# A two-layer hyena, attention and mLSTM model on one core: the recorded stages' issue orders and buffer slots derived anew

## The chip, the cores and the metric

The kernel runs on 1 core of one Trainium2 chip. The metric is the device time of one launch in microseconds (us), as the median of three runs: 1537.01 us for the kernel before, between 1536.03 and 1537.13. Engines are called PE (TensorE, matmuls), DVE (VectorE), ACT (ScalarE), POOL (GpSimd) and SP (SyncE, which here issues nearly all DMA transfers).

## The reference

Two layers run over 512 tokens ("lat") and 256 context tokens ("ctx"), 1024 wide, in fp32. Each layer normalizes its input, scales and shifts it by a modulation of the conditions, mixes, and adds the normalized and gated result. Cut to what matters:

```python
for layer in range(2):
    sh_l, sc_l, ga_l = adaln(c, w_mod[layer], b_mod[layer])      # silu(c) @ w_mod + b_mod, in three parts
    sh_c, sc_c, ga_c = adaln(c_ctx, w_mod[layer], b_mod[layer])
    h_lat = rms_norm(x_lat, g_pre[layer]) * (1 + sc_l) + sh_l    # and h_ctx likewise
    y_lat, y_ctx = even_mixer(...) if layer == 0 else odd_mixer(...)
    x_lat = x_lat + ga_l * rms_norm(y_lat, g_post[layer])        # and x_ctx in layer 0
# even: h @ w_in -> hyena (short conv, gate, long conv by transform) and attention with 8 heads on 2;
#       [hyena * silu(g1), attention * silu(g2)] @ w_out
# odd:  h @ w_in -> mLSTM forward and backward (8 heads, chunks), sum * sigmoid(o), head norm, * silu(z), @ w_out
```

## The kernel before, in words

All large products are emulated in higher precision: each operand is split into a high and a low part (`split`, lines 1024 to 1026: a cast on ACT, then a subtraction on DVE), and `mm3` (line 1034) issues three matmuls, high by high, high by low and low by high, into one PSUM tile.

Weights stream in slices of 256 columns. `load_w` (line 1041) fetches a slice in two halves of 512 KB through three raw buffers (`wr`) and splits each into one of two slots of `wh` and `wl`. While PE reads one slot, the other is refilled. Activations stand in `hTh` and `hTl`, one tile for 512 or 256 tokens.

The modulation is computed by `mod_row`, 256 columns at a time:

```python
for kt in range(KT):
    g = 32 * (kt % 4)
    TE.matmul(ps[g:g + 32], cond[:, kt, :], w[kt], start=kt < 4, stop=kt >= 4)
```

Here `cond` holds the conditions, padded to 32 columns. So each such group is eight plain fp32 matmuls that use a quarter of the array's columns each, in the rows of the profile `128*32`; `w` is an unsplit slice of `w_mod`, held in the place of a `wh` slot (`raw_w`, line 1099). All other matmuls in these stages use the array's full width.

The kernel has seven stages, issued one after the other: "start" (conditions, first norm, first projections), "hy" (hyena), "att" (attention), "out0" (output product of layer 0, its epilogue, and the first transposes of layer 1), "l1a" and "l1b" (layer 1's projections and mLSTM) and "out1" (its output product and epilogue). In a stage `record` (line 1009) only notes the instructions down as the code states them. `play` (line 1014) then issues them by a list of numbers written out in the table `ORDERS` (line 163), and pins that order on every engine:

```python
for i in ORDERS.get(name) or range(len(work)):
    e, fn, a, k = work[i].work
    x = fn(*a, **k)
```

Every engine works its own instructions off in that order, and waits on semaphores where it needs another engine's result or a buffer. Which of a pool's buffers a tile takes is in a second table, `SLOTS` (line 747): `T` (line 949) looks the n-th tile of a tag up there. The PSUM tiles `pj` and `pm` take their slots so, as do `wr`, `xt` and many work tiles. Since every recorded call is issued from one place, nearly all instructions of the profile carry the line 1019.

Of the kernel before, what the change touches and what calls it, by code (L numbers as in the profile page):

```python
# [8 lines left out]
F32R = mybir.dt.float32r  # L9
# [5 lines left out]
P = 128  # L15
# [8 lines left out]
def _hilo(a):  # L24
    """float64 -> two float32 arrays of 12-bit significands whose sum carries 24 bits."""
    a = np.asarray(a, np.float64)

    def r12(v):
        m, e = np.frexp(v)
        return np.ldexp(np.rint(m * 4096.0) / 4096.0, e)  # L30

    hi = r12(a)
    lo = r12(a - hi)
    return hi.astype(np.float32), lo.astype(np.float32)


def _tables():
# [12 lines left out]
    # rotary tables  # L50
# [9 lines left out]
    # hyena positional features, decays and transform matrices, tokens ordered phase by phase  # L60
# [18 lines left out]
    fwd = np.stack([np.cos(ph), -np.sin(ph)], 2)  # tau, r, 2, k  # L79
    iv = np.stack([np.cos(ph), -np.sin(ph)], 2).transpose(3, 1, 2, 0) / NL  # k, r, 2, tau  # L80
    # forward blocks (r, c), then inverse blocks: for c and r = 0, 1 those of r, r + 2 and -(r + 2)
    inv3 = np.stack([iv[:, 0:2], iv[:, 2:4], -iv[:, 2:4]], 3).transpose(0, 2, 1, 3, 4)  # k, c, r, 3, tau
# [5 lines left out]
def _cols(v):  # L88
    """[.., n*128] -> [128, n] columns"""
    v = np.asarray(v)  # L90
    return v.reshape(-1, P).T


def _layout(i):
    """inputs laid out for the device; values unchanged"""
# [16 lines left out]
    def quarters(w):  # L112
        """[1024, 1024] -> [2 groups of 4 k-tiles, 2 column halves, 128, 4 * 512] in the form of a slice"""
        return np.ascontiguousarray(w.reshape(2, 4, P, 2, 512).transpose(0, 3, 2, 1, 4)).reshape(2, 2, P, KT, 256)
# [39 lines left out]
# columns of vecs  # L154
# [3 lines left out]
class Ctx:  # L158
# [3 lines left out]
# the order in which the instructions noted down in a part of the kernel are issued  # L162
# [581 lines left out]
    ],  # L744
}
# which of its buffers a tile takes, by tag and pool
SLOTS = {
    "xt@0": [
        0, 5, 3, 4, 2, 1, 5, 0, 3, 4, 1, 2,
# [6 lines left out]
    ],  # L756
    "ss@0": [
        0, 5, 1, 2, 3, 4,
    ],
    "sst@0": [  # L760
        0, 5, 4, 1, 2, 3,
# [1886 lines left out]
```

## Time and profile before

| what | value |
|---|---|
| median of three runs | 1537.01 us (1536.03 to 1537.13) |
| span of the profiled execution | 1533.4 us |
| between the span and that median | 3.6 us |
| PE busy | 1499.6 us, 98% |
| DVE, ACT, POOL busy | 64%, 47%, 3% |
| HBM traffic | 96 GB/s over the span |

The span runs from the first instruction to the last of one profiled execution. Busy times are sums over an engine's instructions; since matmuls are pipelined and their ends modelled, the step from one matmul's start to the next is a better measure of its cost than its duration. In rows of the timeline the first two numbers are start and duration in us, `x16` counts instructions that a row joins (a plain fp32 matmul shows as two), and brackets name the idle time before a row and who ended it. The stages lie, by PE, at 8.0 to 51.1 us (start), 51.1 to 423.5 (hy), 423.5 to 737.7 (att), 737.7 to 875.3 (out0), 875.3 to 923.5 (l1a), 923.5 to 1434.5 (l1b) and 1434.5 to 1533.4 (out1).

### The profile page before, as it was taken

What the parts mean: (1) busy time and instruction counts of PE and PEld (TensorE: products, weight loads), DVE (VectorE), ACT (ScalarE), POOL (GpSimd) and SP (SyncE); (2) the same over time, 40 slices, a digit from 0 to 9 for tenths busy, and PEclk for the clock granted to TensorE, in tenths of its full rate; (3) what the DMA queues carried; (4) which work ended last, traced back from release to release, by engine and by line L of the source; (5) the groups of instructions that cost most, each with busy time, mean ns of one, the idle gap of its engine ahead of it and who ended that gap; (6) DMA issues with size and microseconds to landing.
All of it is one profiled execution on the core that took longest, in us unless ns stands there. A gap on an engine that the chain in (4) does not pass through costs nothing.

```text
span 1533.4 us, 26152 instructions
## 1 busy us (share of the span) xinstructions
PE 1499.6 (98%) x10652; PEld 1380.3 (90%) x10652; DVE 988.5 (64%) x1947; ACT 716.9 (47%) x1554; POOL 51.7 (3%) x93
## 2 busy tenths in 40 slices
PE   7999999999999999999999899999999999999997
PEld 4889999889999999989988789999999999999885
DVE  6688786877866666684237755665656565666435
ACT  6643444434435454463225566545545453545332
POOL 1000000000000000000001200000000000000000
PEclk9999999999999999999999999999999999999999
DMA  9421211221130111443442402211221232213741
GB/s 375 138 71 51 78 65 51 71 72 39 40 122 29 38 67 61 156 141 105 175 168 97 147 28 87 67 58 63 97 73 56 73 97 73 70 66 104 257 168 69
DMA packets 42625, 148.13 MB, mean 97 GB/s; under 512 B 4928, under 2 KB 7625, under 8 KB 39946
## 3 DMA queue, kind: packets, MB, share of 16 engines
q1 hardware_dynamic: 38968, 137.12, 25.9%
q0 software_dynamic: 1648, 7.01, 1.4%
q10 hardware_dynamic: 1890, 2.34, 0.5%
q8 instruction: 84, 1.38, 0.3%
q14 instruction: 35, 0.29, 0.1%
HBM read 131.77 MB, written 14.68 MB: 96 GB/s over the span
## 4 chain that ended last, share of the span: by engine, by line
PE 93%; ACT 2%; DVE 2%; issue 1%; DMA 1%; SPq 0%; POOL 0%; POOLq 0%; DVEq 0%; ACTq 0%
PE pj L1019 77%; PE pm L1019 14%; PE s L1019 2%; ACT wh L1019 1%; DMA dfb<-y_scratch 1%; DMA xt<-in_x 0%; DVE wl L1019 0%; DVE hTl L1019 0%; ACT hf L1019 0%; ACT hTh L1019 0%; ACT q L1019 0%; DVE hf L1019 0%; DVE xn L1019 0%; DVE xnT L1019 0%; SPq L1019 0%
## 5 line engine op out<-in xcount | busy, mean ns | idle before, releaser
L1019 PE MATMUL pj<-wh,hTh 128*128 128x256 f32 (+1 forms) x1536 | 442.9, 289 | 3.3 <-ACT wh L1019 3.0
L1019 PE MATMUL pj<-wl,hTh 128*128 128x256 f32 (+1 forms) x1536 | 438.3, 285 | 3.2 <-DVE wl L1019 2.1
L1019 PE MATMUL pj<-wh,hTl 128*128 128x256 f32 (+1 forms) x1536 | 437.8, 285 | 0.0
L1019 PEld LDWEIGHTS pj<-wh,hTh 128*128 128x128 f32 x1536 | 290.0, 189 | 9.4 <-ACT wh L1019 4.3
L1019 PEld LDWEIGHTS pj<-wl,hTh 128*128 128x128 f32 x1536 | 291.5, 190 | 6.6 <-DVE wl L1019 4.3
L1019 PEld LDWEIGHTS pj<-wh,hTl 128*128 128x128 f32 x1536 | 290.9, 189 | 1.4
L1019 PE MATMUL pj<-hTh,wh 128*128 128x512 f32 (+1 forms) x832 | 287.1, 345 | 0.0
L1019 PE MATMUL pj<-hTh,wl 128*128 128x512 f32 (+1 forms) x832 | 285.3, 343 | 0.5 <-DVE wl L1019 0.5
L1019 PE MATMUL pj<-hTl,wh 128*128 128x512 f32 (+1 forms) x832 | 285.3, 343 | 0.5 <-DVE hTl L1019 0.5
L1019 DVE TENSOR_TENSOR wl<-wr,wh 128x1024 fp32r<-128x1024 f32 x148 | 180.1, 1218 | 77.4 <-ACT wh L1019 77.1
L1019 ACT CAST wh<-wr 128x1024 fp32r<-128x1024 f32 x148 | 154.1, 1049 | 72.4 <-PE pj L1019 49.3
L1019 PEld LDWEIGHTS pj<-hTh,wl 128*128 128x128 f32 x832 | 156.7, 188 | 21.2 <-DVE wl L1019 0.9
L1019 PEld LDWEIGHTS pj<-hTh,wh 128*128 128x128 f32 x832 | 156.8, 188 | 19.2 <-issue 0.8
L1019 PEld LDWEIGHTS pj<-hTl,wh 128*128 128x128 f32 x832 | 156.8, 188 | 19.0 <-DVE hTl L1019 0.8
L1019 DVE TENSOR_TENSOR PTl<-pj,PTh 128x384 fp32r<-128x384 f32 (+1 forms) x80 | 40.9, 523 | 21.5 <-ACT PTh L1019 21.4
L1019 ACT CAST PTh<-pj 128x384 fp32r<-128x384 f32 (+1 forms) x80 | 35.1, 459 | 40.9 <-PE pj L1019 38.5
L1019 DVE SCALAR_TENSOR_TENSOR C<-C,apb,pj 128x258 f32<-128x258 f32 x64 | 30.6, 479 | 31.2 <-PE pj L1019 30.2
L1019 DVE TENSOR_TENSOR Cl<-C,Ch 128x258 fp32r<-128x258 f32 x64 | 26.8, 423 | 37.1 <-ACT Ch L1019 36.8
L1019 DVE SCALAR_TENSOR_TENSOR num<-pm,cq,num 128x258 f32<-128x258 f32 x64 | 30.2, 480 | 25.4 <-PE pm L1019 10.9
L1019 PE MATMUL pm<-Rh,dfa 128*128 128x256 f32 (+1 forms) x192 | 44.7, 304 | 0.0
L1019 DVE TENSOR_REDUCE mx<-s 128x1 f32<-128x768 f32 (+1 forms) x48 | 36.9, 771 | 11.2 <-PE s L1019 11.2
L1019 DVE TENSOR_TENSOR med<-big 128x512 f32<-128x512 f32 (+1 forms) x48 | 40.4, 864 | 4.8 <-ACT big L1019 4.6
(341 smaller groups left out, 2725.3 us busy)
## 6 DMA issues: line engine op xcount, KB each, us to landing
wr<-in_o_w_in SPq DMA_DIRECT2D x64, 512.0 KB
wr<-in_e_w_in SPq DMA_DIRECT2D x52, 512.0 KB
wh<-in_w_mod SPq DMA_DIRECT2D x18, 1024.0 KB
wr<-in_e_w_out SPq DMA_DIRECT2D x16, 512.0 KB
wr<-in_o_w_out SPq DMA_DIRECT2D x16, 512.0 KB
xt<-in_x SPq DMA_DIRECT2D x12, 512.0 KB
y_scratch<-y SPq DMA_DIRECT2D x8, 512.0 KB
xt<-in_w_mod SPq DMA_DIRECT2D x6, 512.0 KB
```

Source lines behind the costliest of these rows:

```text
L1019: x = fn(*a, **k)
```

## The change

The two tables are replaced; nothing else of the code's statements differs. `ORDERS["start"]` stays as it was. In the other six stages the same numbers stand in another order: 3158 recorded instructions in hy, 3143 in att, 1037 in out0, 426 in l1a, 5281 in l1b and 675 in out1. On the average an instruction moves by 30 to 40 places, at most by several hundred. `SLOTS` has new slots for nearly every tag. Instructions, transfers and buffers are the same in kind and number. The line of the calls becomes 1022, as the tables are three lines longer. A line of each table's diff:

```diff
-        0, 5, 3, 4, 2, 1, 5, 0, 3, 4, 1, 2,
+        2, 3, 1, 4, 5, 0, 3, 2, 1, 0, 4, 5,
...
-        0, 2, 1, 0, 2, 1, 0, 2, 1, 0, 2, 1, 0, 2, 1, 0, 2, 1, 0, 2, 1, 0, 2, 1, 0, 2, 1, 0, 2, 1, 0, 2, 1, 0, 2, 1, 0, 2, 1, 0, 2, 1, 0, 2, 1, 0, 2,
+        2, 0, 2, 1, 1, 0, 1, 0, 1, 2, 1, 0, 2, 1, 0, 2, 0, 2, 1, 0, 0, 2, 2, 0, 1, 2, 0, 0, 2, 1, 0, 2, 2, 0, 2, 1, 0, 1, 2, 1, 0, 2, 0, 2, 0, 1, 1,
```

The first place is on PE near the end of att, around one group of modulation matmuls (`pj_4816<-wh_1174,cond`; `PTh`, `PTl` are the attention's weights, `hTh`, `hTl` the activations). Before:

```order
L1019 MATMUL pj_4814<-PTh_4807,hw_1049 128x256
L1019 MATMUL pj_4814<-PTl_4808,hw_1049 128x256
L1019 MATMUL pj_4814<-PTh_4807,ab_1050 128x256
L1019 MATMUL pj_4816<-wh_1174_4810,cond_67 32x256 x8
L1019 MATMUL pj_4815<-wh_1129_4765,hTh 128x256
L1019 MATMUL pj_4815<-wl_1130_4766,hTh 128x256
```

And now:

```order
L1022 MATMUL pj_4806<-PTh_4792,hw_1049 128x256
L1022 MATMUL pj_4816<-wh_1174_4810,cond_67 32x256 x4
L1022 MATMUL pj_4806<-PTl_4793,hw_1049 128x256
L1022 MATMUL pj_4813<-wh_1129_4765,hTl 128x256
L1022 MATMUL pj_4816<-wh_1174_4810,cond_67 32x256
L1022 MATMUL pj_4806<-PTh_4792,ab_1050 128x256
L1022 MATMUL pj_4816<-wh_1174_4810,cond_67 32x256
L1022 MATMUL pj_4821<-wh_1129_4765,hTl 128x256
L1022 MATMUL pj_4816<-wh_1174_4810,cond_67 32x256
L1022 MATMUL pj_4821<-wh_1129_4765,hTh 128x256
```

The group of eight, once together, is now dealt out among products of three other tiles; its last matmul follows some rows further down. Of the 16 groups outside the first stage 16 runs stood on PE before (8 in att, 4 in out0, 4 in out1), and 43 stand now (26, 10 and 7).

The second place is on PE in the first part of l1b, where a projection tile `pj_10005`, the mLSTM's sums `pm_9997`, and the next projection tile `pj_10019` stand. Before:

```order
L1019 MATMUL pj_10005<-wl_1695_9963,hTh 128x256
L1019 MATMUL pj_10005<-wh_1694_9962,hTl 128x256
L1019 MATMUL pm_9997<-Ch_9988,qh_9948 128x258
L1019 MATMUL pm_9997<-Cl_9989,qh_9948 128x258
L1019 MATMUL pm_9997<-Ch_9988,ql_9949 128x258
L1019 MATMUL pj_10019<-wh_1700_9968,hTh 128x256
```

And now:

```order
L1022 MATMUL pm_9997<-Cl_9989,qh_9948 128x258
L1022 MATMUL pj_10005<-wh_1694_9962,hTl 128x256
L1022 MATMUL pj_10023<-vh_9921,kah_10017 128x258
L1022 MATMUL pj_10031<-wh_1700_9968,hTh 128x256
L1022 MATMUL pm_9997<-Ch_9988,ql_9949 128x258
L1022 MATMUL pm_10012<-ncs_9219,pick_9220 128x512
L1022 MATMUL pj_10023<-vl_9922,kah_10017 128x258
L1022 MATMUL pj_10019<-wh_1700_9968,hTh 128x256
```

The products of several tiles now alternate, matmul by matmul, and `pj_10019`, which has the slot of `pj_10005`, begins five matmuls behind that tile's last one.

The third place is the end of the program on SP's queue, where the result is stored (`xt_16105`, `xt_16110`, `xt_16116` and `xt_16122` are the four token blocks, each in two halves). Before:

```order
L1019 DMA out_x<-xt_16105 128x512
L1019 DMA out_x<-xt_16116 128x512 x2
L1019 DMA out_x<-xt_16105 128x512
L1019 DMA out_x<-xt_16122 128x512 x2
L1019 DMA out_x<-xt_16110 128x512 x2
```

And now:

```order
L1022 DMA out_x<-xt_16110 128x512
L1022 DMA out_x<-xt_16105 128x512 x2
L1022 DMA out_x<-xt_16116 128x512 x2
L1022 DMA out_x<-xt_16110 128x512
L1022 DMA out_x<-xt_16122 128x512 x2
```

The two stores of `xt_16122` are now the last on the queue, where those of `xt_16110` were.

More of the change, by code (lines that the diff above doesn't have):

```diff
@@ L748 @@
     "xt@0": [
-        0, 5, 3, 4, 2, 1, 5, 0, 3, 4, 1, 2,
+        2, 3, 1, 4, 5, 0, 3, 2, 1, 0, 4, 5,
     ],
     "wr@1": [
[4 rows of a table removed]
[4 rows of a table added]
     ],
     "ss@0": [
-        0, 5, 1, 2, 3, 4,
+        0, 1, 2, 3, 4, 5,
     ],
     "sst@0": [
-        0, 5, 4, 1, 2, 3,
+        0, 1, 3, 4, 2, 5,
     ],
     "rs@0": [
-        0, 5, 4, 1, 2, 3,
+        0, 1, 4, 3, 2, 5,
     ],
     "pj@2": [
-        0, 3, 2, 1, 0, 3, 2, 1, 0, 3, 2, 1, 0, 3, 2, 1, 0, 3, 2, 1, 0, 3, 2, 1, 0, 3, 2, 1, 0, 3, 2, 1, 0, 3, 2, 1, 0, 3, 2, 1, 0, 3, 2, 1, 0, 3, 2,
-        1, 0, 3, 2, 1, 0, 3, 2, 1, 0, 3, 2, 1, 0, 3, 2, 1, 0, 3, 2, 1, 0, 3, 2, 1,
+        1, 3, 1, 3, 0, 2, 2, 3, 0, 1, 2, 1, 3, 0, 1, 0, 3, 2, 1, 0, 3, 2, 3, 2, 0, 1, 2, 1, 3, 0, 2, 1, 3, 1, 1, 3, 2, 0, 3, 1, 0, 2, 1, 2, 3, 0, 0,
+        2, 3, 1, 0, 2, 3, 1, 1, 2, 3, 0, 0, 2, 1, 1, 1, 2, 3, 3, 2, 3, 1, 0, 3, 2,
     ],
     "xn@0": [
-        0, 2, 1, 2, 0, 2,
+        0, 1, 1, 2, 0, 2,
     ],
     "pm@3": [
[4 rows of a table removed]
[4 rows of a table added]
     ],
     "mrow@4": [
-        0, 3, 1, 2, 0, 3, 2, 1, 3, 0, 2, 1, 3, 0, 2, 1, 3, 0, 2, 1, 3, 0, 2, 1,
+        2, 3, 0, 1, 2, 3, 0, 1, 2, 3, 0, 1, 2, 3, 0, 1, 2, 0, 1, 3, 0, 2, 1, 3,
     ],
     "g@5": [
-        0, 1, 0, 1, 0, 1, 0, 1,
+        1, 0, 1, 0, 1, 0, 1, 0,
     ],
     "x0s@5": [
-        0, 1, 0, 1, 0, 1, 0, 1,
+        1, 0, 1, 0, 1, 0, 1, 0,
     ],
@@ L791 @@
     "med@5": [
[3 rows of a table removed]
[3 rows of a table added]
     ],
     "big@5": [
-        1, 0, 0, 0, 1, 1, 1, 0, 0, 0, 1, 1, 1, 0, 0, 0, 1, 1, 1, 0, 0, 0, 1, 1,
+        1, 0, 1, 1, 0, 1, 1, 0, 1, 1, 0, 1, 1, 0, 1, 1, 0, 1, 1, 0, 1, 1, 0, 1,
     ],
     "rt@6": [
-        0, 1, 0, 1, 0, 1, 0, 1, 0, 1, 0, 1, 0, 1, 0, 1, 0, 1, 0, 1, 0, 1,
+        1, 1, 0, 1, 1, 1, 1, 0, 0, 1, 1, 0, 1, 0, 1, 0, 0, 1, 1, 0, 1, 1,
     ],
@@ L808 @@
     "qTh@6": [
-        0, 0, 2, 1, 0, 2, 1, 0, 2,
+        0, 0, 1, 2, 0, 1, 2, 0, 1,
     ],
@@ L824 @@
     "rq@6": [
-        0, 3, 1, 2, 0,
+        3, 0, 1, 2, 3,
     ],
     "s2@8": [
-        0, 1, 0, 1, 0, 1, 0, 1, 0, 1, 0, 1, 0, 1, 0, 1, 0, 1, 0, 1, 0, 1, 0, 1, 0, 1, 0, 1, 0, 1, 0, 1, 0, 1, 0, 1, 0, 1, 0, 1, 0, 1, 0, 1, 0, 1, 0, 1,
+        1, 0, 0, 1, 1, 0, 1, 0, 1, 0, 1, 1, 0, 1, 1, 0, 0, 1, 0, 0, 1, 0, 0, 1, 0, 1, 1, 0, 1, 0, 1, 0, 1, 1, 0, 0, 1, 0, 1, 0, 1, 1, 0, 1, 0, 1, 1,
+        0,
     ],
     "mx@6": [
-        0, 3, 2, 1, 0, 3, 2, 1, 0, 3, 2, 1, 0, 3, 2, 1, 0, 3, 2, 1, 0, 3, 2, 1, 0, 3, 2, 1, 0, 3, 2, 1, 0, 3, 2, 1, 0, 3, 2, 1, 0, 3, 2, 1, 0, 3, 2, 1,
+        3, 0, 2, 1, 0, 3, 1, 2, 3, 0, 2, 1, 3, 0, 1, 2, 3, 0, 2, 3, 1, 0, 2, 3, 1, 0, 2, 3, 1, 0, 2, 3, 1, 0, 2, 3, 1, 0, 2, 3, 1, 0, 2, 3, 1, 0, 3,
+        2,
     ],
     "sm@6": [
-        0, 3, 2, 1, 0, 3, 2, 1, 0, 3, 2, 1, 0, 3, 2, 1, 0, 3, 2, 1, 0, 3, 2, 1, 0, 3, 2, 1, 0, 3, 2, 1, 0, 3, 2, 1, 0, 3, 2, 1, 0, 3, 2, 1, 0, 3, 2, 1,
+        3, 0, 1, 2, 0, 3, 2, 1, 0, 3, 2, 1, 0, 3, 1, 2, 0, 3, 1, 2, 0, 3, 1, 2, 0, 3, 1, 2, 0, 3, 1, 2, 3, 0, 1, 2, 3, 0, 1, 2, 0, 3, 1, 2, 0, 3, 2,
+        1,
     ],
@@ L839 @@
     "pj@10": [
[6 rows of a table removed]
[6 rows of a table added]
     ],
     "pm@11": [
[5 rows of a table removed]
[5 rows of a table added]
     ],
     "yraw@9": [
-        0, 1, 0, 1, 0, 1, 0, 1,
+        0, 0, 1, 0, 1, 0, 0, 1,
     ],
     "ess@9": [
-        0, 1, 0, 1, 0, 1,
+        0, 0, 0, 0, 0, 0,
     ],
@@ L869 @@
     "xn@9": [
-        0, 2, 1, 0, 2, 1, 0, 2, 1, 0, 2, 1,
+        0, 1, 1, 2, 0, 2, 1, 0, 2, 1, 0, 1,
     ],
@@ L878 @@
     "cvo@12": [
-        0, 1, 1, 0, 1, 0, 1, 0, 1, 0, 1, 0, 1, 0, 1, 0, 1, 0,
+        0, 1, 0, 1, 1, 0, 1, 0, 1, 0, 1, 0, 0, 1, 1, 0, 0, 1,
     ],
     "vh@12": [
-        0, 1, 0, 1, 0, 1, 0, 1, 0,
+        0, 1, 0, 0, 1, 0, 1, 0, 1,
     ],
     "vl@12": [
-        0, 1, 0, 1, 0, 1, 0, 1, 0,
+        0, 0, 1, 0, 1, 0, 1, 1, 0,
     ],
     "hn@12": [
-        0, 1, 0, 1, 0, 1, 0, 1,
+        1, 0, 1, 0, 1, 0, 1, 0,
     ],
     "C@13": [
-        0, 1, 0, 1, 0, 1, 0, 1, 0, 1, 0, 1, 0, 1, 0, 1, 0, 1, 0, 1, 0, 1, 0, 1, 0, 1, 0, 1, 0, 1, 0, 1, 0, 1, 0, 1, 0, 1, 0, 1, 0, 1, 0, 1, 0, 1, 0,
-        1, 0, 1, 0, 1, 0, 1, 0, 1, 0, 1, 0, 1, 0, 1, 0, 1, 0, 1, 0, 1, 0, 1, 0, 1, 0, 1, 0, 1, 0, 1, 0, 1,
+        0, 1, 0, 1, 0, 1, 0, 1, 0, 1, 0, 1, 0, 1, 0, 1, 0, 1, 0, 1, 0, 1, 0, 1, 0, 0, 1, 0, 1, 0, 0, 1, 0, 1, 0, 1, 0, 1, 0, 1, 1, 0, 1, 0, 1, 0, 1,
+        0, 1, 0, 1, 0, 1, 0, 1, 0, 1, 0, 1, 0, 1, 0, 1, 0, 1, 0, 1, 0, 1, 0, 0, 1, 0, 1, 0, 1, 0, 1, 0, 1,
     ],
     "Ch@13": [
-        0, 1, 0, 1, 0, 1, 0, 1, 0, 1, 0, 1, 0, 1, 0, 1, 0, 1, 0, 1, 0, 1, 0, 1, 0, 1, 0, 1, 0, 1, 0, 1, 0, 1, 0, 1, 0, 1, 0, 1, 0, 1, 0, 1, 0, 1, 0,
-        1, 0, 1, 0, 1, 0, 1, 0, 1, 0, 1, 0, 1, 0, 1, 0, 1,
+        0, 1, 0, 1, 0, 1, 0, 0, 1, 0, 1, 0, 1, 1, 0, 1, 0, 1, 0, 1, 0, 1, 1, 0, 0, 1, 0, 1, 1, 0, 1, 0, 0, 1, 0, 1, 0, 1, 1, 0, 0, 1, 0, 1, 0, 1, 0,
+        1, 0, 0, 1, 0, 1, 0, 0, 1, 1, 1, 0, 1, 0, 1, 1, 0,
     ],
     "Cl@13": [
-        0, 1, 0, 1, 0, 1, 0, 1, 0, 1, 0, 1, 0, 1, 0, 1, 0, 1, 0, 1, 0, 1, 0, 1, 0, 1, 0, 1, 0, 1, 0, 1, 0, 1, 0, 1, 0, 1, 0, 1, 0, 1, 0, 1, 0, 1, 0,
-        1, 0, 1, 0, 1, 0, 1, 0, 1, 0, 1, 0, 1, 0, 1, 0, 1,
+        1, 0, 1, 0, 0, 0, 1, 1, 1, 0, 1, 0, 1, 1, 0, 0, 1, 0, 1, 0, 1, 0, 0, 1, 1, 0, 1, 0, 0, 1, 1, 0, 0, 1, 0, 1, 0, 1, 1, 0, 1, 0, 1, 0, 1, 0, 0,
+        1, 0, 0, 1, 0, 1, 0, 0, 1, 1, 1, 0, 1, 0, 1, 1, 0,
     ],
     "dn@13": [
-        0, 3, 1, 2, 0, 3, 1, 2, 0, 3, 1, 2, 0, 3, 1, 2,
+        3, 1, 3, 1, 3, 1, 3, 1, 3, 3, 3, 1, 3, 3, 3, 3,
     ],
     "yraw2@14": [
-        0, 3, 2, 1, 0, 3, 2, 1,
+        2, 0, 1, 3, 0, 2, 3, 1,
     ],
     "ess@14": [
-        0, 1, 0, 1,
+        0, 0, 0, 0,
     ],
@@ L917 @@
     "xt@14": [
-        0, 3, 2, 1,
+        3, 2, 1, 0,
     ],
```

1160 rows, old and new, of tables (ORDERS, SLOTS) are left out of this document.

## The prediction

> **What bounds the kernel now.** I read the page first, then the windows by stage, then PE's waits, then single places.
>
> ```profile
> span 1533.4 us, 26152 instructions
> PE 1499.6 (98%) x10652; PEld 1380.3 (90%) x10652; DVE 988.5 (64%) x1947; ACT 716.9 (47%) x1554; POOL 51.7 (3%) x93
> ```
>
> TensorE (PE) is busy for 98% of the span, and no other compute engine above 64%. The windows, cut at the stages' ends, tell where the rest lies. The first column after the window is its length, the second PE's busy time:
>
> ```profile
> 51.10:423.50 372.40, 371.90 (x2386) 338.69 (x2385) 290.30 (x469) 156.21 (x252) 1.64 (x3) 1.00 0.18 61
> 423.50:737.70 314.20, 313.10 (x2413) 292.73 (x2412) 194.87 (x480) 144.61 (x387) 14.37 (x9) 1.00 0.27 94
> 737.70:875.30 137.60, 131.23 (x802) 112.86 (x803) 80.16 (x142) 58.05 (x115) 14.90 (x27) 0.98 0.42 145
> 875.30:923.50 48.20, 45.43 (x287) 39.02 (x285) 26.57 (x57) 31.37 (x57) 0.55 (x1) 1.00 0.15 47
> 923.50:1434.50 511.00, 509.24 (x3911) 491.38 (x3913) 317.15 (x666) 262.20 (x635) 9.94 (x29) 1.00 0.24 78
> 1434.50:1533.40 98.90, 87.84 (x553) 75.44 (x552) 42.34 (x62) 29.78 (x57) 3.16 (x4) 0.95 0.47 165
> ```
>
> PE idles 0.5 us in hy, 1.1 in att, 6.4 in out0, 2.8 in l1a, 1.8 in l1b and 11.1 in out1. Of out1's, 9.9 are the tail behind the last matmul (1523.48, quoted below). So new orders can at most give back 0.5 + 1.1 + 6.4 + 2.8 + 1.8 + 1.2 = 13.8 us of waits and a little of the tail; the rest of the time is matmuls, whose set doesn't change. PE's waits over the stages out0 and l1a, then over l1b and out1 (total us, times, longest):
>
> ```profile
> PE pm L1019 <- DVE xn L1019: 3.2, 3, 1.8
> PE pj L1019 <- DVE wl L1019: 2.2, 4, 0.7
> PE pj L1019 <- ACT wh L1019: 1.8, 2, 1.1
> ```
>
> ```profile
> PE pm L1019 <- DVE hh L1019: 1.2, 1, 1.2
> PE pj L1019 <- ACT wh L1019: 1.2, 1, 1.2
> PE pj L1019 <- DVE zs L1019: 0.4, 1, 0.4
> ```
>
> **What the order removes: waits.** The rows of the places on which the gains rest, PE's first, then VectorE's (DVE), GpSimd's (POOL) and SyncE's queue:
>
> ```profile
> 680.43 1.07 PE L1019 MATMUL pj<-wh,cond 128*32 128x256 f32 x16 [0.66 <-DVE dec L1019]
> 739.87 0.39 PE L1019 MATMUL pj<-wl,hTh 128*128 128x256 f32 x1 [0.74 <-DVE wl L1019]
> 868.24 0.63 PE L1019 MATMUL pm<-c_ident,xn 128*128 128x128 f32 x4 [1.80 <-DVE xn L1019]
> 1424.30 1.56 PE L1019 MATMUL pm<-c_ident,hh 128*128 128x128 f32 x8 [1.25 <-DVE hh L1019]
> 1523.48 0.40 PE L1019 MATMUL pj<-wh,ycl 128*128 128x512 f32 x1
> ```
>
> ```profile
> 848.92 0.48 DVE L1019 TENSOR_SCALAR xn<-xt,rs 128x512 f32<-128x512 f32 x1
> 865.31 4.08 DVE L1019 TENSOR_SCALAR xn<-xt,rs 128x512 f32<-128x512 f32 x2
> 1526.84 1.41 DVE L1019 SCALAR_TENSOR_TENSOR xt<-yacc,ers,xt 128x512 f32<-128x512 f32 x2 [0.44 <-POOL ers L1019]
> ```
>
> ```profile
> 863.92 0.96 POOL L1019 MEMSET gwh<- 128x1024 f32 x1
> ```
>
> ```profile
> 1525.29 4.79 SPq L1019 DMA_DIRECT2D out_x<-xt  x7
> ```
>
> (Work ahead of a point is counted in the two orders, at 0.12 us a matmul of 256 columns; that step is read from rows below.) At 680 the new order spreads the eight cond matmuls out and has other work around them: -1.0 of the stage's 1.1 (the 0.66 and what small waits there are beside it). At the start of out0 the last read of the weight slot stands 2.2 us of matmuls ahead of the first read of its new content, where it was 1.3: the 0.74 goes, -0.7. Before the transposes of hh at the end of l1b the order has 7.9 us of PE work where it had 6.1 since the last product that hh needs: the 1.25 and the 0.4 of zs go, and I take -1.8, all that l1b idles. In l1a the first read of a slice's new content moves 0.3 us away from the last of the old one, -0.3. At the end of out0 the chain that leads to xn (y sum, squares, scale, x, squares, scale) is set by DVE, ScalarE (ACT) and POOL, and PE only fills it: PE has 35 matmuls of 0.12 us left behind the last transposes where it had 44, so -1.0. xn itself took 4.08 us for two while POOL wrote constants (the first of them is the row at 863.92), 0.48 for one elsewhere; one constant more now stands ahead there, +0.5 (0 to 0.8). At the end SP used to issue the last two stores of xt_16110 behind those of xt_16122, and xt_16122 now goes last: of the 4.79 us of queued stores about 1.0 leaves the end. DVE's last xt ends at 1528.25, so no more than the queue behind it is to be had. The weights' first wait in out1 (1.2) stays, since the first read still stands right behind the last use of its slot. Sum of the waits: -1.0 - 0.7 - 1.8 - 0.3 - 1.0 - 1.0 + 0.5 = **-5.3 us**.
>
> **What it adds: breaks in the cond matmuls.** These products use 32 columns of the array (the form 128*32). Each group of eight stood together outside the first stage. First a group of 8, then one of 16 in the first stage, and for comparison 8 full-width transposes:
>
> ```profile
> 730.25 0.28 PE L1019 MATMUL pj<-wh,hTl 128*128 128x256 f32 x1
> 730.45 1.07 PE L1019 MATMUL pj<-wh,cond 128*32 128x256 f32 x16
> 731.46 0.39 PE L1019 MATMUL pj<-wh,hTh 128*128 128x256 f32 x1
> 731.68 0.28 PE L1019 MATMUL pj<-wl,hTh 128*128 128x256 f32 x1
> 731.79 0.28 PE L1019 MATMUL pj<-wh,hTl 128*128 128x256 f32 x1
> ```
>
> ```profile
> 36.42 0.28 PE L1019 MATMUL pj<-hTh,wl 128*128 128x256 f32 x1
> 36.63 1.50 PE L1019 MATMUL pm<-dfa,cond 128*32 128x256 f32 x24
> 37.95 0.61 PE L1019 MATMUL pm<-dfb,cond 128*32 128x256 f32 x8
> 38.84 0.40 PE L1019 MATMUL pj<-hTl,wh 128*128 128x512 f32 x1
> 39.07 0.39 PE L1019 MATMUL pj<-hTh,wl 128*128 128x512 f32 x1
> ```
>
> ```profile
> 852.00 0.39 PE L1019 MATMUL pj<-wh,yol 128*128 128x512 f32 x1
> 852.23 1.04 PE L1019 MATMUL pm<-c_ident,xn 128*128 128x128 f32 x8
> 853.23 0.28 PE L1019 MATMUL pj<-wl,hTh 128*128 128x256 f32 x1
> ```
>
> The step between two plain matmuls is 0.12 us (731.68 to 731.79) at 256 columns and 0.23 (38.84 to 39.07) at 512. From 730.25 to 731.68 are 1.43 us; less two steps of 0.12, eight cond matmuls cost 1.19. From 36.42 to 38.84 are 2.42; less 0.12 and 0.23, sixteen cost 2.07. Eight more cost 0.88, or 0.11 each, so going in and out costs 1.19 - 0.88 = 0.31 us a run. For the transposes, 1.23 less 0.23 and 0.12 is 0.88, again 0.11 each: I take it that a full-width run pays nothing at its edges. In the new order the 16 groups outside the first stage fall into 43 runs (att 26, out0 10, out1 7). 27 runs more by 0.31 are **+8.4 us**, all on PE, which waits nowhere at most of these places. No trace here shows a single cond matmul. 22 runs are of odd length; if an odd one costs as much as a pair, each adds 0.11 (+2.4); at worst every new edge loses as much as two matmuls (27 by 0.22, +5.9); at best nothing. I take **+2**.
>
> The Trainium skill's page "TensorEngine Tiling (Array Packing)", section "Tiling Modes", says that changing the tiling mode drains TensorE and that different tiles can work in parallel. By that rule the edge's price belongs to every change between the full and the 32-column form, and a matmul alone also loses its neighbours; the trace agrees with 0.31 us in and out, and no run here shows the second.
>
> **What it adds: tight PSUM slots.** The new order deals products of several output tiles in turn (in l1b the tile changes 1332 times along PE, before 406). That alone costs nothing by these rows: a step into another tile is 0.12 too. But a slot is now refilled sooner. PE work between the last product into a slot's old tile and the first into its new one, by 0.12 us a matmul, is under 1.0 us at 56 places outside the first stage (before 5; of these 28 in l1b, 13 in att). What has to fit in is seen here:
>
> ```profile
> 1058.06 0.28 PE L1019 MATMUL pj<-wh,hTl 128*128 128x256 f32 x1
> ...
> 1058.38 0.38 ACT L1019 ACTIVATE so<-pj 128x256 f32<-128x256 f32 x1 [1.97 <-PE pj L1019]
> ```
>
> 0.32 us from the last product's start to the reader, which takes 0.38, so 0.70 and a release: the new order leaves 0.69 to 0.72 at its tightest. It fits if the reader's engine is free, and costs up to one more operation of 0.38 if not. 51 more such places by 0 to 0.16 us (under half such an operation) are 0 to +8; I take **+2**, nearer the free end, as DVE and ACT are busy 64% and 47%.
>
> **Sum.** 8.4 + 2 - 5.3 + 2 = +7.1 us on the span of 1533.4, so 1540.5. The median of the runs, 1537.0, lies 3.6 above the span; I keep that: **1544 us**.
>
> **Rivals.**
>
> Faster: the edge's price is of the first stage's and the long groups' making (a wait for the slice's landing that the records don't show), not of every run. Then the waits go for nothing: 1537.0 - 5.3 + 0 to 2, about **1532**. It decides from 5.3 / 27 = 0.20 us a run downward. For it: in att PE is idle beside some groups; against: 0.31 comes out of two groups in which PE waited for nothing. Chance 0.18. The page's rule above speaks against it.
>
> No change: edges cost 0.31 only where PE doesn't wait, single ones nothing extra, and slots fit: 8.4 - 5.3 less about 2 that falls into waits, +1, or **1538**. Chance 0.13.
>
> Much slower: the readers of the tight slots are late as a rule, by 0.25 us at each of 51 places, most of them in l1b and att, because ACT and DVE work in program order and a cast of weights may stand ahead: +13 in place of +2, **1555**. Against: the engines have room on average. Chance 0.14.
>
> That leaves 0.55 for the forecast. All stages' orders do change, so a change without effect is not among them.
>
> The range: forecast's unknowns are cond (0 to 5.9 instead of 2) and slots (0 to 8 instead of 2), so 1540 to 1554; the rivals on both sides widen it to **1531 to 1559**, leaving out the faster one's lower half and the last of the much slower one. About 0.2% (3.1 us) is what a measurement can tell from no change. Faster by more 0.18, within 0.13, slower by more 0.69.
>
> **What would show it.** Right: att's window without PE waits but some 5 to 7 us longer, the cond rows in 43 groups with 0.4 us from the last plain matmul to the next for a single one; l1b within 3 us of before; PE waits on so, num, C and PTh of 0.1 to 0.4 us each; the hh wait gone. Wrong: single cond matmuls at 0.12 us; or att shorter than 314 us; or l1b longer by over 5 us, which would be the tight slots.

## The result, and the profile after

The changed kernel takes 1571.89 us (1569.6 to 1572.58, four runs), the kernel before 1536.55 in the same session: a ratio of 1.023, with a 95% interval of 1.0216 to 1.0245. So it is 35 us slower, where 7 were forecast, and outside the range given. Its profiled execution took 1569.6 us, of which the page shows the span:

```profile
span 1567.5 us, 26223 instructions
PE 1528.1 (97%) x10652; PEld 1387.0 (88%) x10652; DVE 1011.5 (65%) x1947; ACT 728.1 (46%) x1554; POOL 51.7 (3%) x93
```

TensorE's busy time has grown by 28.5 us with the same 10652 matmul records, and its idle time from 33.8 to 39.4. The windows by stage (length, then PE's busy time; near the end the mean granted clock) say where:

```profile
50.60:422.90 372.30, 371.06 (x2385) 337.93 (x2383) 297.42 (x472) 158.68 (x255) 1.64 (x3) 1.00 0.20 61
422.90:765.10 342.20, 333.70 (x2414) 298.96 (x2414) 202.33 (x478) 150.53 (x389) 14.28 (x9) 0.99 0.25 84
765.10:910.80 145.70, 137.25 (x802) 113.36 (x802) 78.82 (x144) 57.58 (x114) 15.60 (x30) 0.98 0.40 137
910.80:959.20 48.40, 46.59 (x287) 40.51 (x287) 26.21 (x56) 29.46 (x52) 0.00 (x0) 0.96 0.24 70
959.20:1469.10 509.90, 509.59 (x3910) 491.21 (x3908) 327.35 (x667) 269.51 (x642) 10.60 (x26) 1.00 0.25 76
1469.10:1567.50 98.40, 88.91 (x553) 74.63 (x552) 42.82 (x62) 29.63 (x56) 2.53 (x4) 0.98 0.48 168
```

Set beside those of before: hy 372.3 us as before (372.4), att 342.2 (314.2), out0 145.7 (137.6), l1a 48.4 (48.2), l1b 509.9 (511.0), out1 98.4 (98.9). Att has lost 28.0 us and out0 8.1; the stage with the most tight PSUM slots, l1b, has won 1.1 and its PE now idles 0.3 us.

The cond matmuls are the first thing to read. PE's timeline in att, at runs of one, three, four and again one matmul (a cond matmul shows as two):

```profile
695.42 0.62 PE L1022 MATMUL pj<-wh,cond 128*32 128x256 f32 x2
695.98 0.55 PE L1022 MATMUL pj<-c_ident,hdl 128*128 128x128 f32 x3
...
699.09 1.05 PE L1022 MATMUL pj<-wh,cond 128*32 128x256 f32 x6
700.08 0.39 PE L1022 MATMUL s<-dfa,qTl 128*128 128x256 f32 x1
...
700.74 0.64 PE L1022 MATMUL pj<-wh,cond 128*32 128x256 f32 x8
701.31 0.33 PE L1022 MATMUL pj<-c_ident,hdh 128*128 128x128 f32 x1
...
704.08 0.62 PE L1022 MATMUL pj<-wh,cond 128*32 128x256 f32 x2
704.63 0.50 PE L1022 MATMUL s<-dfa,qTh 128*128 128x512 f32 x1
```

From a run's first start to the next matmul's, one matmul takes 0.56 us, three 0.99, four 0.57, one 0.55; eight took 1.01 in the trace of before (730.45 to 731.46). So the time doesn't go by the number. It goes by the column group that the run uses most often: the four at 700.74 use each group once, of the three at 699.09 two use group 0. All 43 runs fit 0.12 + 0.43 us for each time that the busiest column group comes up, which I call a round (0.55 to 0.57 for one round, 0.98 to 1.02 for two; one run that ends in a wait aside). The group of 16 in the first stage, 36.63 to 38.50, is four rounds: 1.87. The 16 groups had 32 rounds before; in 43 runs they have 70.

The second thing is what PE waits for, in att and then in out0:

```profile
PE pj L1022 <- ACT qjunk L1022: 4.2, 4, 2.8
PE pj L1022 <- DVE qTl L1022: 1.9, 1, 1.9
PE pj L1022 <- DVE rt L1022: 1.8, 2, 1.2
PE pj L1022 <- ACT hdl L1022: 1.3, 1, 1.3
PE pj L1022 <- DVE PTh L1022: 0.4, 1, 0.4
```

```profile
PE pm L1022 <- ACT hf L1022: 6.0, 4, 2.7
PE pm L1022 <- DVE hf L1022: 1.2, 1, 1.2
PE pm L1022 <- DVE xn L1022: 1.1, 2, 0.6
```

None of the first list was there before; the second has taken the place of 6.4 us of other waits. Behind such waits the granted clock falls, here in att:

```profile
455.00:461.80 6.80, 5.81 (x27) 5.81 (x28) 2.48 (x8) 2.71 (x12) 0.00 (x0) 0.50 0.25 75
```

The clock is 0.50 for 6.8 us. PE's 27 matmuls from 455.99 us to the end of this window took 5.81 us; in the version with three tiles' reads moved (below), at clock 1.00, the same 27 took 3.44 us beside a wait of 1.09. So about 2.4 us are lost here. In out0 such a stretch of 6.8 us stands in both kernels, from 888.5 us now and from 857.9 before.

And the end of the program, SP's queue and DVE's last rows:

```profile
1559.33 0.39 PE L1022 MATMUL pj<-wh,ycl 128*128 128x512 f32 x1
1559.51 5.24 SPq L1022 DMA_DIRECT2D out_x<-xt  x5
1562.98 1.42 DVE L1022 SCALAR_TENSOR_TENSOR xt<-yacc,ers,xt 128x512 f32<-128x512 f32 x2 [0.44 <-POOL ers L1022]
```

From the last matmul to the span's end are 8.2 us, before 9.9.

### The profile page after: what moved, and what is told of

Read it like the earlier page. It is cut to its first block, busy times and chain, and to the rows that moved or that the text cites. A ratio compares the mean times of both kernels' runs of the same rounds, so it can differ in the third digit from the quotient of the medians.

```text
span 1567.5 us, 26223 instructions
## 1 busy us (share of the span) xinstructions
PE 1528.1 (97%) x10652; PEld 1387.0 (88%) x10652; DVE 1011.5 (65%) x1947; ACT 728.1 (46%) x1554; POOL 51.7 (3%) x93
## 5 line engine op out<-in xcount | busy, mean ns | idle before, releaser
L1022 PE MATMUL pj<-wh,hTh 128*128 128x256 f32 (+1 forms) x1536 | 426.2, 289 | 6.4 <-ACT wh L1022 2.0
L1022 PE MATMUL pj<-wl,hTh 128*128 128x256 f32 (+1 forms) x1536 | 428.8, 288 | 1.1 <-DVE wl L1022 1.1
L1022 PE MATMUL pj<-wh,hTl 128*128 128x256 f32 (+1 forms) x1536 | 425.8, 288 | 0.2 <-DVE hTl L1022 0.2
L1022 PEld LDWEIGHTS pj<-wh,hTh 128*128 128x128 f32 x1536 | 286.8, 190 | 15.5 <-issue 5.3
L1022 PEld LDWEIGHTS pj<-wh,hTl 128*128 128x128 f32 x1536 | 287.0, 190 | 5.8 <-issue 2.5
L1022 PE MATMUL pj<-hTh,wh 128*128 128x512 f32 (+1 forms) x832 | 282.2, 346 | 1.9 <-DVE qTl L1022 1.9
L1022 PE MATMUL pj<-hTh,wl 128*128 128x512 f32 (+1 forms) x832 | 280.8, 344 | 0.3 <-DVE wl L1022 0.3
L1022 ACT CAST PTh<-pj 128x384 fp32r<-128x384 f32 (+1 forms) x80 | 35.3, 459 | 52.0 <-PE pj L1022 51.8
L1022 DVE SCALAR_TENSOR_TENSOR cvo<-pj,cv,cvo 128x511 f32<-128x511 f32 (+1 forms) x48 | 31.6, 659 | 28.2 <-ACT cvo L1022 27.4
L1022 PE MATMUL s<-dfa,qTh 128*128 128x256 f32 (+1 forms) x160 | 45.8, 341 | 0.0
```

## The experiments

Theory A after this reading: the split cond groups cost 27 more edges of 0.31 us and 38 more rounds of 0.43, together 24.7; the rest is that reads and writes of one PSUM tile by different engines stand in an unlucky order, in att and out0. Theory B is the prediction's other term: slots refilled too soon, and products of several tiles in turn.

**Groups together.** Of the 16 groups' numbers those of one, at the end of att:

```diff
-... 3039, 3038, 3042, 3037, 2941, 2983, 3041, 2853, 2942, 3036, 3080, 3040, 3081, ... 2944, 2945, 3043, 3044
+... 2941, 2983, 2853, 2942, 3080, 3081, ... 2944, 2945, 3036, 3037, 3038, 3039, 3040, 3041, 3042, 3043, 3044
```

> The changed kernel, with each of the 16 groups of eight cond matmuls outside the first stage put together again at the place of its last one; nothing else moves. Theory A (a run of cond matmuls costs 0.31 us at its edges and 0.43 us for each round of up to four different column groups, and the split groups need 70 rounds in 43 runs where 32 in 16 do): 27 * 0.31 + 38 * 0.43 = 24.7 us come back, so about 1547 us. Theory B (a matmul costs 0.11 us in any run, 0.31 us at the edges; the rest of the loss is tight PSUM slots and alternating tiles in att and out0): 8 to 10 us come back, so about 1562.

Measured: 1549.82 us, a ratio to before of 1.0092 (1.0077 to 1.0107). 22.1 us came back, near A's 24.7 and far from B's 8 to 10. Att went from 342.2 to 328.9, out0 from 145.7 to 142.8. In the trace PE idles 9.7 us in att, where it idled 8.5, and 10.8 in out0, where it idled 8.5: a part of the saved time went into waits.

**Pairs of the same columns, and of different ones**, in the kernel before; one group of att as it was, with either edit:

```diff
-1981, 1982, 1961, 1983, 1984, 1985, 1986, 1987, 1994, 1995, 1996, 2012, 1997, 2013, 2014, 2015, 2016, ... 2017, 2018, 2019
+1981, 2012, 2016, 1982, 1961, 1983, 1984, 2013, 2017, 1985, 1986, 1987, 2014, 2018, 1994, 1995, 1996, 2015, 2019, 1997
+1981, 2012, 2013, 1982, 1961, 1983, 1984, 2014, 2015, 1985, 1986, 1987, 2016, 2017, 1994, 1995, 1996, 2018, 2019, 1997
```

> The kernel before, with 12 of its 16 groups of cond matmuls dealt into four pairs, three or four other matmuls between them, each pair of the same column group (k-tiles 0 and 4, 1 and 5, and so on). Theory A: each pair is two rounds, so a group costs 4 * (0.31 + 0.86) instead of 1.17: 12 * 3.51 = 42 us more, about 1579. Theory B (0.31 us at the edges, 0.11 for a matmul): 12 * 3 * 0.31 = 11 us more, about 1548.

> The same 12 groups of the kernel before at the same places in four pairs, but each pair of two different column groups (k-tiles 0 and 1, 2 and 3, and so on). Theory A: each pair is one round, so a group costs 4 * (0.31 + 0.43) instead of 1.17: 12 * 1.79 = 21 us more, about 1558, 21 us less than with pairs of the same columns. Theory B: as with pairs of the same columns, about 1548.

Measured, one run each: 1579.03 and 1555.52 us, against 1535.77 for the kernel before: 43.3 and 19.8 us more, where A had 42 and 21 and B 11 for both. Pairs of the same columns, and then of different ones, in PE's timeline:

```profile
560.38 1.05 PE L1023 MATMUL pj<-wh,cond 128*32 128x256 f32 x4
561.36 0.74 PE L1023 MATMUL s<-dfa,qTh 128*128 128x512 f32 x2
```

```profile
558.41 0.63 PE L1023 MATMUL pj<-wh,cond 128*32 128x256 f32 x4
```

Two matmuls in both, 0.98 us in the first and in the second 0.56 by the same reading. The two kernels differ by 48 rounds alone, so 23.5 us is 0.49 a round, where A had 0.43. With this the price of a round is shown by a run; that of an edge was not varied alone.

**The instructions that wait for rq.** In att's rotary part the new order has DVE's product with rq (number 229) two places behind POOL's computation of rq (190, 2.30 us in the profile), and DVE's whole queue behind it. On the kernel with the groups together:

```diff
-187, 189, 190, 161, 229, 329, 188, 263, 330, 226, 4, 223, 44, 232, 228, ... 231, ... 5, 225, ... 271, 219, 272
+187, 189, 190, 161, 329, 188, 263, 330, 4, 44, ... 5, ... 271, 219, 229, 226, 223, 232, 228, 231, 225, 272
```

> As the kernel with the groups put together, and in addition the seven instructions near the start of att that wait for rq from GpSimd are issued behind the three reads of pj_4287 by VectorE, where they stood right behind rq's computation, ahead of the queue of VectorE's and ScalarE's rotary work. Theory A (VectorE stands for 2.2 us at rq with all that work behind it, TensorE then waits for PSUM slots by 1.3 and 2.8 us and is clocked down for 7 us): 5 to 8 us less than the kernel with the groups put together, att's first waits and the slower clock gone. Theory B (the slots of att are too tight in themselves): within 2 us of it.

Measured: 1548.49 us, 1.3 below the kernel that it is built on, which as a time is B's. In the two traces PE reaches the same matmul 3.1 us earlier from 470 us on and keeps that to the end of out0; it then loses 1.1 in l1a. So A's cause is there in att, at about half its size: of the waits of 1.25 and 2.77 us the first went, the second became 2.29, and 3.4 of 6.8 us at the half clock stayed.

**ScalarE's reads first.** After that PE waited for qjunk. DVE's and ACT's reads of one rotary tile stand in the trace so (DVE and ACT of the changed kernel, tile pj_4287):

```profile
450.71 0.28 ACT L1022 ACTIVATE qjunk<-pj 128x128 f32<-128x128 f32 x1 [2.49 <-DVE dfb L1022]
...
451.43 0.28 ACT L1022 ACTIVATE qjunk<-pj 128x128 f32<-128x128 f32 x1 [0.36 <-DVE rt L1022]
```

```profile
451.11 0.29 DVE L1022 TENSOR_TENSOR rt<-pj,cs 128x128 f32<-128x128 f32 x1 [0.30 <-ACT qjunk L1022]
451.83 0.29 DVE L1022 TENSOR_TENSOR rt<-pj,cs 128x128 f32<-128x128 f32 x1 [0.43 <-ACT qjunk L1022]
```

Both only read the tile, and still each waits for the other's read that was issued before. ACT's first read waited 2.49 us so. After it a read takes 0.28 or 0.29 us, 0.03 to 0.12 pass from the end of one engine's read to the start of the other's, and each engine stands idle for 0.30 to 0.43 us at every turn. The Trainium skill's page "PSUM — Partial Sum Buffer", section "PSUM bank collisions raise a hardware error", says that two engines' accesses to one bank need a dependency, reads and writes alike; the waits of ACT for DVE's read (0.36) and of DVE for ACT's (0.30, 0.43) agree.

First I moved ACT's reads ahead in 25 tiles, and one split of weights (332, 333) behind:

```diff
-217, 215, 250, 251, ... 261, 218, 264, 265, 266, 267, 216, 268, ...
+215, 216, 217, 250, 251, ... 257, 258, 261, 218, 264, 265, 266, 267, 268, ...
```

> The kernel with the groups together and the rq instructions moved, and in addition, in att, ScalarE's reads (qjunk) of each rotary tile in PSUM issued ahead of VectorE's reads of the same tile (25 tiles), and one split of a weight slice behind VectorE's reads of pj_4291. Theory A (an engine's read of a PSUM tile waits for the other engine's earlier issued read of it, so ScalarE stood behind VectorE's queue and the slot came free late): att 325.7 us becomes 321 to 323, so 3 to 5 us less than the kernel it is built on, about 1544. Theory B (VectorE and ScalarE are just full there): within 1 us of 1548.

Measured: 1548.43 us, the time of the kernel that it is built on, as B said. But the trace doesn't show engines that are just full. Against the kernel with the groups alone 5.4 us were won by the matmul at 460 us, 2.9 of them by rq, and by 600 us all of it was lost again, mostly at a wait of 2.0 us for hdh at 565 with half a clock behind it. So att ends 2.9 us later than without the edit of the reads, and out0, which is 2.5 us shorter, hides it.

**Transposes together.** In out0 four transposes of xn fill a PSUM tile, and ACT and DVE read it in four parts. At six places a transpose now comes behind a read of its own tile; before, at one. Here the first three of one tile, PE's rows and then ACT's, of the changed kernel:

```profile
885.41 0.33 PE L1022 MATMUL pm<-c_ident,xn 128*128 128x128 f32 x1
887.41 0.33 PE L1022 MATMUL pm<-c_ident,xn 128*128 128x128 f32 x1 [1.32 <-ACT hf L1022]
890.41 0.48 PE L1022 MATMUL pm<-c_ident,xn 128*128 128x128 f32 x1 [2.67 <-ACT hf L1022]
```

```profile
885.63 1.03 ACT L1022 CAST wh<-wr 128x1024 fp32r<-128x1024 f32 x1
886.56 0.80 ACT L1022 ACTIVATE hf<-pm,shf,scl 128x128 f32<-128x128 f32 x2
888.86 1.06 ACT L1022 ACTIVATE junk<-xt 128x1024 f32<-128x1024 f32 x1 [1.50 <-issue]
...
889.92 0.44 ACT L1022 ACTIVATE hf<-pm,shf,scl 128x128 f32<-128x128 f32 x1
```

The second transpose waits for a read (886.56) that stands behind a cast of weights on ACT; the third waits for one (889.92) behind the sum of squares. The edit, at that tile, on the kernel with the groups together:

```diff
-853, 995, 858, 862, 965, 966, 967, ... 831, 859, 863, 940, 860, 968, ... 886, 880, 861, 855
+853, 995, 858, 859, 860, 861, 862, 965, 966, 967, ... 831, 863, 940, 968, ... 886, 880, 855
```

> The changed kernel with the cond groups together, and in out0 the four transposes of xn into each of four PSUM tiles (pm_8097, pm_8142, pm_8155, pm_8159) issued together at the place of the first; the new order has six of these transposes behind a read of the same tile, the old one had one. Theory A (TensorE waits for that read, 1.3, 2.7 and 1.8 us in the profile, and runs at half clock behind it): out0 142.7 us becomes 137 to 139, so about 1545. Theory B (the chain of the epilogue on VectorE, ScalarE and GpSimd sets out0's end): out0 stays within 1 us of 142.7, about 1549.

Measured: 1544.49 us (1.0057 of before, 1.0041 to 1.0072), 5.3 below the kernel that it is built on. Out0 fell from 142.8 to 134.9 us, 2.7 below before. PE's waits there:

```profile
PE pj L1023 <- ACT hTh L1023: 2.6, 1, 2.6
PE pm L1023 <- DVE xn L1023: 1.5, 2, 1.0
PE pj L1023 <- DVE hTl L1023: 0.2, 1, 0.2
```

The waits for hf are gone. A holds, by more than it said; a part is not its own, since the last two xn take 2.39 us together in this trace and 3.74 in that of the kernel that it is built on.

**Three tiles only**, with groups, transposes and rq moved: of the reads' edit only tiles 4287, 4291 and 4295.

> The changed kernel with cond groups and out0's transposes together and the rq instructions moved, and ScalarE's reads ahead of VectorE's for the three rotary tiles alone (pj_4287, pj_4291, pj_4295) at which TensorE waited. Moving them for 25 tiles had won 5.4 us by TensorE's matmul at 460 us and lost it again at other tiles by 600. Theory A (a read that is issued behind another engine's read of its PSUM tile waits for it): 3.5 to 5.5 us below the kernel with groups and transposes together, about 1540. Theory B (att's rotary part is bound by VectorE's work): 0 to 3.2 us below it, as rq alone.

Measured: 1541.53 us, 3.0 below the kernel with groups and transposes, so as a time within B's range. In the trace att is 4.2 us shorter at its end, of which rq alone had given 3.2 on the kernel with the groups; the three tiles' reads give the other 1.0, which is too little to tell the theories apart.

**The second rq**, the same pattern at the first score block (464 to 467 wait for rq):

```diff
-403, 404, 463, 464, 465, 466, 467, 443, 454, 427, 455, 456, ... 469, 413, 414, 472
+403, 404, 463, 443, 454, 427, 455, 456, ... 469, 413, 414, 464, 465, 466, 467, 472
```

> The kernel with groups, transposes, the first rq instructions and the three tiles' reads moved, and in addition the four instructions of the first score block that wait for the second rq (mx, hdl, sm, hdl) issued behind the two qTh and qTl reads of PSUM that stood behind them. Theory A (VectorE and ScalarE stand for 1.5 and 1.9 us at the second rq with the reads behind them, and TensorE waits 1.86 us for the slot and is clocked down behind it): 1.5 to 3.5 us less in att. Theory B (the reads wait for their own inputs, or the score block that is now later is waited for instead): within 0.7 us.

Measured: 1541.69 us, the same as without. In the trace att is 1.0 us shorter, its clock no longer falls, and of the wait of 1.86 us for qTl there remain 0.8 and 1.0 for the scores: the wait was passed on, as B said.

**Stages of both kernels.** Hy, l1a, l1b and out1 of the changed kernel, att and out0 of before, by the tables' parts:

> Orders and slots of hy, l1a, l1b and out1 from the changed kernel (out1's cond groups together), those of att and out0 from the kernel before. Theory A (alternating tiles and tight PSUM slots cost nothing, att and out0 hold all the loss): hy 0, l1a -0.4, l1b -1.1, out1 -3.2 us, so about 4 to 5 us below the kernel before. Theory B (part of the loss lies in tight slots everywhere, and was only passed on): equal to the kernel before or above it.

Measured: 1540.53 us, 4.8 above before. But it is the seam that cost it: the first stage, whose order is the same in all kernels, took 50.3 us instead of 43.1 and hy 374.7 instead of 372.3, since the slot numbers of the first stage were of one table and hy's of the other. So it says nothing on A or B. With out1 alone:

> The kernel before with out1 alone from the changed kernel, its cond groups together. Theory A (out1's own new order, its last stores above all, is worth what its window showed): 2.5 to 3.2 us below the kernel before. Theory B (out1's gain came from what l1b left for it): 0 to 1 us below.

Measured: 1533.98 us, a ratio of 0.9987 (0.9978 to 0.9995), 1.8 us below, between the theories; the interval, 0.8 to 3.4 us, reaches into both. In the trace out1 is 3.3 us shorter, as A said, and the first stage, which was not changed, 1.3 longer. With the seam mended:

> As the mix of the changed kernel's hy, l1a, l1b and out1 (cond groups together) with att and out0 of the kernel before, but with the first stage's slots from the changed kernel too, so that hy's slots follow on those that they were derived with: in the first mix the first stage took 7.2 us longer and hy 2.4, which is the seam of the two slot tables. Theory A (alternating tiles and tight PSUM slots cost nothing): 3 to 5 us below the kernel before. Theory B (they cost something in those stages): equal or above.

Measured: **1529.6 us, a ratio of 0.9955 (0.9941 to 0.9969)**: 6.6 us below the kernel before, more than A said, and the fastest version of all. Only slots of the first stage differ from the first mix, so the seam is shown. Its windows:

```profile
50.90:423.00 372.10, 371.10 (x2385) 337.92 (x2383) 297.17 (x472) 158.60 (x255) 1.63 (x3) 1.00 0.20 61
423.00:737.30 314.30, 313.23 (x2413) 292.87 (x2413) 195.02 (x479) 146.09 (x389) 14.38 (x9) 1.00 0.28 92
737.30:872.90 135.60, 131.01 (x802) 112.93 (x802) 78.30 (x142) 57.97 (x115) 16.25 (x30) 0.97 0.43 146
...
921.10:1430.90 509.80, 509.48 (x3908) 491.12 (x3906) 327.26 (x667) 269.59 (x641) 10.62 (x26) 1.00 0.24 76
1430.90:1528.10 97.20, 87.73 (x553) 75.17 (x552) 42.81 (x62) 29.64 (x56) 2.54 (x4) 0.96 0.49 170
```

Hy, with products of several tiles in turn, is as long as ever, and l1b is shorter: alternating tiles and the tight slots cost nothing there. Out0 is 2.0 us shorter, though its order and slots are those of before: VectorE's last two xn took 2.19 us together, where the kernel before took the 4.08 shown in the prediction. Last, att alone from before, and out0 new too, with its transposes together:

> Everything from the changed kernel but att's order and slots, which are those of before; the cond groups together, and the transposes of out0's four tiles together. Theory A (the loss is the split cond groups, the transposes behind reads in out0, and att's rotary start): out0 135 us, l1b 510, out1 3 us shorter, so 5 to 7 us below the kernel before, about 1530. Theory B (out0's gain was made by the late start that att gave it): 2 to 4 below, as the other mix.

Measured: 1532.48 us, 0.9976 (0.9967 to 0.9985), 3.7 below the kernel before, as B said. It beats the kernel before, but not the other mix: out0 took 136.7 us here and 135.6 there, in a run that was the fastest of eleven. So the new out0, mended, is no better than the old.

## Why the prediction was wrong, point by point

**Edges of the cond runs: right, as far as the runs tell.** 27 more edges by 0.31 us, +8.4, stand in A's sum, and that sum met three experiments within 2.6 us. No run had other edges and the same rounds.

**The cond matmuls inside a run: the step that failed.** The prediction took 0.88 us for eight more matmuls, divided by eight, and put 0.11 on a matmul in any run; for single ones it took +2, at worst +5.9. But the eight more were two rounds of 0.43, in which four column groups run side by side. A matmul alone takes a whole round. 38 more rounds are 16.3 us, not 2. What it would have needed stood in the code and in the trace of before. `mod_row` puts k-tile kt into column group kt % 4. In the trace four of the 16 records of the group at 730.45 start within 0.02 us, and the next four 0.22 us behind them; the timeline joins them into one row. No second length of run was there to divide by except the one of 16, which is a whole number of rounds too. The page "TensorEngine Tiling (Array Packing)" of the Trainium skill was cited in the prediction for tiles that work in parallel, and the price that follows from it was left at 0.22 a break. The Trainium skill's page "TensorE: Matmul & The Clock Gate", section "Measured speedup vs the span model", says that matmuls in different tiles take one duration and some 4 ns for each further one; the trace agrees, 0.55 us for one and 0.57 for four.

**Tight PSUM slots: a late reader did cost time, but hardly where the prediction counted.** In l1b with its 28 such places PE idles 0.3 us in all, and inside hy it waits at none. PE waits at one tight place alone, where att begins: the new tile's first product stands right behind the old tile's last one, and ACT comes to its read of the old tile (`hdl`) only behind a cast. PE's rows and then ACT's:

```profile
421.38 0.28 PE L1022 MATMUL pj<-wh,hTl 128*128 128x256 f32 x1
422.94 0.39 PE L1022 MATMUL pj<-wh,hTh 128*128 128x256 f32 x1 [1.27 <-ACT hdl L1022]
```

```profile
421.51 0.83 ACT L1022 CAST hw<-hdh 128x768 fp32r<-128x768 f32 x1
422.24 0.64 ACT L1022 COPY hdl<-pj 128x256 f32<-128x256 f32 x2
```

So of the +2, 1.3 us came. The other waits of att's list, up to the 2.8 us for qjunk, stand at refilled slots too, but there 1.3 to 6.1 us of PE work lie between the slot's old tile and its new one, counted as in the prediction. Distance on PE alone was the wrong thing to count. What cost most is the order between engines on one tile: a transpose behind a read of its tile (out0), and a read behind another engine's read, whose engine stands at something else (att). Neither shows when one counts from a slot's last product to its next first one.

**The waits: -5.3 was forecast, they became more.** l1b gave its 1.1 of 1.8, the first wait of out0 went (0.7 as forecast), 680's wait went, and the tail gave 1.7 us for 1.0. But the end of out0, put at -1.0, got 2.1 us more idle time, and att 7.4 more. For xn it added 0.5, and there the new order was better: the last two took 2.00 us where they had taken 4.08, and PE waited 1.1 us for xn where it had waited 3.2. The 1.2 in out1 stayed, as forecast. The prediction looked at the places where the old order waited and saw most of them mended; it didn't look for new ones by the same reading in ACT's and DVE's orders.

**The clock: not in the sum.** 2.4 us in att are lost to the half clock behind two waits.

**The signs.** Of those for a right forecast, l1b within 3 us came true, and the wait for hh shrank from 1.2 to 0.2 us. Att was to have no waits of PE and to be 5 to 7 us longer; it has 8.5 us of idle time and is 28.0 us longer.

Where the 35.3 us went, by the runs: the cond groups 22.1; out0's transposes 5.3; rq and the three tiles in att 3.0. That leaves 1541.5 us, 5.3 above before in that session. In its trace att is still some 10 us longer than before, against gains elsewhere. PE idles 6.8 us there, where it idled 1.1, at about ten waits of 0.3 to 1.9 us, and 3.4 us pass at half clock. A wait also costs more than its bracket says: at the one shown above, PE's next start behind 422.94 is at 423.16. From 421.38 that is 1.78 us; less two steps of 0.12 and the bracket's 1.27 there remain 0.27. By an estimate from these rows, ten waits make 3 us of that. Two of att's causes were tried and gave 3.2 and 1.0 us, a third passed its wait on. What sets the other waits off was not tried and stays open; that they go with att's order and slots is shown by the mix, where att has those of before and takes 314.3 us.

**The rivals.** The much slower one ended on the right side, in part by luck: most of the loss is in the cond groups, whose extra rounds it doesn't have, and l1b, where most of its places lie, got shorter. But its words "in program order" and "a cast may stand ahead" fit the wait at the start of att, and out0's transposes too, though those don't stand in a refilled slot.

## What to carry to other kernels

Price an operation by the smallest and the largest group in which the trace shows it, and ask what runs side by side inside a group before dividing by its number; an order that is made with a fixed cost for each matmul of a small tile can take a group apart for nothing and pay a whole round for each piece. When an order is derived anew, check for every PSUM tile that all its writes come ahead of its first read (5.3 us in out0), and that nothing long, such as a wait for a slow engine or a cast, stands ahead of the reads that free it. One engine's reads in one piece were worth 1.0 us at three tiles and lost time at 25, so move them only where TensorE waits. And when stages of two such tables are mixed, take the buffer slots of neighbouring stages from one table.

## What the runs showed of the hardware that was not expected

- A run of 32-column matmuls (256 columns of data, fp32) takes 0.12 + 0.43 us for each matmul in the column group that it uses most, whatever the order inside: 0.55 for one, 0.57 for four in four groups, 0.98 for two in one group, 1.01 for eight in four groups.
- Taking turns, matmul by matmul, between the accumulations of several full-width PSUM tiles cost nothing in hy and l1b: hy's 372.3 us didn't move when its tile changes went from 194 to 754, and l1b's 1332 changes came with 1.1 us less.
- Two short waits of PE, 1.25 and 2.77 us, within 5 us brought 6.8 us at half clock; in the variant with the second rq moved, a wait of 1.1 us, ending at 454.7, and waits of 0.8 and 1.0, ending at 471.9 and 475.0, brought none.
